# A second Strassen level inside two of the seven products of an MLP's first matrix product, for four pairs of output blocks

## The chip, the cores and the metric

The kernel runs on one core of one Trainium2 chip. The metric is the device time of one execution in microseconds (us). The engines are named as in the profile: PE (TensorE matmuls), PEld (its weight loads), DVE (VectorE), ACT (ScalarE), POOL (GpSimd) and SP (SyncE, which issues all DMAs here). DVE, ACT, POOL and SP each work through one list of instructions in the order of the program; an instruction waits until the semaphores it names have come, and what stands behind it on the same engine waits with it.

## The reference

One encoder layer on 1024 tokens of width 1024. Attention and a short convolution come first; the change lies in the last line.

```python
u = rms_norm(x, norm1_g); proj = u @ w_in          # q k v cb cc ch ga gb
...                                                # neighbourhood attention, gated conv, branches, gates
x = x + merged @ w_o                               # (1024, 1024)
h = rms_norm(x, norm2_g) @ w_mlp_in                # (1024, 4096)   "first MLP product"
x = x + jnp.square(jax.nn.relu(h)) @ w_mlp_out     # (1024, 1024)   "second MLP product"
```

Inputs and outputs are float32. A float32 operand is split into a high and a low float16 half, and a product is done in three passes (high·high, high·low, low·high; `PASSES`).

## The kernel before

**Strassen.** The first MLP product is computed as a 2x2 block product by a form of Strassen with seven products instead of eight. The tokens are cut into two halves of 512, the 1024 inner columns into two halves of 512, and the 4096 outputs into two halves of 2048. The seven forms of the activations (`fv`, `U2`, made once per 128 tokens by `sums`, `high`, `low` and DMA transposes) are shared by 16 blocks `q` of 128 + 128 output channels. For each block the weights (two raw tiles of 512 KB) become seven forms as well:

1. `rows_scaled`: ACT multiplies the raw rows by the norm's gain (8 instructions, in place); `squares`: two ACT squares with a row sum.
2. `sum_of`: DVE sums the two columns and casts the result into a column of `ones`; PE multiplies it by a matrix of ones (`all_sum`, line 227, a matmul with one column, to which the text refers as the *ones matmul*), and DVE makes a power-of-two scale of it (`pow2_half`).
3. `forms_sum`: POOL adds four weight forms (`tsum`); `forms_split` with `parts`: ACT writes the high halves (line 1238), DVE the low halves (line 1234) into `P1[q]`, one of three rotating buffers (`TAGS`).
4. `quad(q)`: seven groups of 4 x 3 matmuls of 128x512, each into one of the eight PSUM banks (`anybank` takes them in turn), 84 matmuls per block. DVE and ACT read the banks back into `AS[q]` (lines 1740 to 1761).
5. `h_done(q)`: ACT relu and square (2048 columns each), POOL four sums, and a store of 1.8 MB to the DRAM tensor `HS`.

Blocks 0 and 1 run in two halves of 256 tokens, since the last activation forms are still being made.

**What sets the order.** Python generators. `unit` emits a group of matmuls, then steps the foreground list `fg` (`step`) and the background list `bg` (`tick`) a few times; each `yield` gives the place to the next. So one fixed order per engine comes out of the interleaving. `gate(q)` holds back the writing of a weight buffer until the block that used it has been emitted, and `apart` keeps a ones matmul some matmuls behind its operand in the program. `X1` holds the residual, 128 x 8 x 1024 float32, and stays in place until the second MLP product adds to it.

Of the kernel before, what the change touches and what calls it, by code (L numbers as in the profile page):

```python
# [18 lines left out]
D = 1024  # L19
# [80 lines left out]
def encoder_block(ctx: ExitStack, tc: tile.TileContext, x, weights, cols, gqk, rel, masks, out):  # L100
# [282 lines left out]
    g1, g2, gm2 = at(consts, 0, 8), at(consts, 20, 8), keep()  # L383
    rows = {"A": lambda j: rowsA, "B": lambda j: rowsB, "O": lambda j: rowsM}
    chunks, offset = {}, 0
    for (kind, j), pieces in plan():
        ch = chunks[kind, j] = Chunk(kind, [(nk, sum(n for _, n in cs)) for _, _, nk, cs in pieces],
                                     {"A": "wa", "B": "wb"}.get(kind, "ws"), rows.get(kind, lambda j: g1)(j),
                                     j if kind == "V" else None, 9 if kind in "VQKCGS" else 0)
        ch.first = len(loads)  # L390
        for p, (k, w) in enumerate(ch.widths):
            ch.offs.append(offset)
            if kind != "X" and (kind, j) != ("1", 0) and (kind, j, p) != ("1", 1, 1):
                loads.append((ch, p))
            offset += 128 * k * w
# [1031 lines left out]

    pair_done, fv, ssq = [0], [], keep(10)

# [6 lines left out]
    def row_scale(col, n=1):  # L1436
        y = tmp(n)
        for _ in rstd(at(ssq, col, n), D, y, 9):
            pass
        return y  # L1440
# [5 lines left out]
    def begin(n):  # L1446
# [5 lines left out]
        for i in range(2):  # L1452
            normal(n + 4 * i, at(y, i))

    PART = ((0, 4), (4, 7))
# [62 lines left out]
    def prep1(q):  # L1518
# [7 lines left out]
        ready.add(q)  # L1526
        if 1 < q < 15:
            yield from sums1(q + 1)

    SQJ = U2[1][:, 0, :, :, 384:512].rearrange("p s k t -> p (s k) t").bitcast(BF16)  # L1530
# [20 lines left out]
    def forms_m():  # L1551
# [101 lines left out]
    def do(f, *a):  # L1653
        return lambda: f(*a)
# [12 lines left out]
    tail(3, 0, sq(6), do(low, 1, 0), lambda: y.append(row_scale(4, 2)), do(high, 1, 1),  # L1667
         lambda: (normal(2, at(y[0], 0)), normal(6, at(y[0], 1))), do(low, 1, 1))
# [3 lines left out]
    tail(7, 1, sq(3, 1), g1, lambda: normal(3, row3(3)), g1)  # L1672
    fv[1] = wsp.tile([128, 7, 2, 512], F16, name="v16", tag="ws")

    def last_pair():
# [51 lines left out]
    def quad(q, c0=0, c1=512):  # L1727
        need(q)
        if c0 == 0:
            while q - 2 in live:  # L1730
                step()
            live.add(q)
            AS[q] = w4p.tile([128, 7, 512], F32, name="as", tag="as")
        ps = {}
# [17 lines left out]
        def post3(ps):  # L1752
# [9 lines left out]
            7: post7, 3: post3}, 2 if c1 == 512 else 3, 5, (1, 2, 5, 4, 6, 7, 3) if c0 else (1, 6, 5, 4, 2, 7, 3))  # L1762

    def whole(q):
        quad(q)
        pe_done[0] = q + 1
# [9 lines left out]
    held[0] = 0  # L1776
    for q in range(2, 14):
        whole(q)


# [109 lines left out]
    bg.append(prep2(0))  # L1890
    whole(14)
    pace[0] = 1
    whole(15)
# [133 lines left out]
```

## Time and profile before

| | |
|---|---|
| median of 3 runs | 1201.6 us (1201.53 to 1202.12) |
| profiled execution, its own time | 1201.36 us |
| its span on the core | 1199.6 us, so 1.8 us lie around the span |
| granted TensorE clock | 1.00 |
| busy: PE, DVE, ACT, POOL | 1190.7, 937.1, 752.1, 450.5 us |
| instructions | 16983, of them 6272 matmuls |

The trace is of one execution. A busy PE is no proof of a PE at its peak, since matmuls overlap in the pipeline: the distance between the starts of two groups tells what a group costs. A row of the timeline gives start, length, engine, line, operation, output and inputs with their shapes, and behind it in brackets the time that the engine sat idle before it and who released it.

### The profile page before, as it was taken

To read this page: it belongs to the slowest core of one execution; us is meant where nothing else is said; L and a number is where in the kernel's file an instruction comes from. 1 tells how busy PE (TensorE), PEld (TensorE's weight loads), DVE (VectorE), ACT (ScalarE), POOL (GpSimd) and SP (SyncE) were. 2 spreads that over 40 slices of the span, in tenths; PEclk is the share of its full clock that TensorE was granted. 3 is DMA by queue.
4 is the path that set the end of the run, shared out by engine and by line. 5 is a ranking of instruction groups with operands and counts; after the bars stand their busy time and mean duration, and the time that the engine had idled before them with its cause. 6 is when DMAs were issued, how large, how long until landed. Compare 5 with 4: busy or idle time off the path is not lost.

```text
span 1199.6 us, 16983 instructions
## 1 busy us (share of the span) xinstructions
PE 1190.7 (99%) x6272; PEld 575.5 (48%) x6272; DVE 937.1 (78%) x1750; ACT 752.1 (63%) x1181; POOL 450.5 (38%) x296
## 2 busy tenths in 40 slices
PE   8999999999999999999999999999999999999998
PEld 7444444445444444444467444444444444444444
DVE  7987878899558786877888645645648999999998
ACT  7765668778654544336778778778575843746440
POOL 5610022322321213001014666565567561554562
PEclk9999999999999999999999999999999999999999
DMA  7745547687641121233396545535466925335302
GB/s 262 197 154 125 110 96 143 123 163 128 131 119 56 51 71 36 71 132 149 68 168 195 172 146 184 166 125 192 157 238 223 354 72 207 144 130 204 105 36 105
DMA packets 162707, 171.25 MB, mean 143 GB/s; under 512 B 123328, under 2 KB 123840, under 8 KB 158528
## 3 DMA queue, kind: packets, MB, share of 16 engines
q1 hardware_dynamic: 162624, 170.17, 48.7%
q8 instruction: 49, 0.80, 0.3%
q14 instruction: 34, 0.28, 0.1%
HBM read 102.51 MB, written 37.75 MB: 117 GB/s over the span
## 4 chain that ended last, share of the span: by engine, by line
PE 91%; DVE 6%; ACT 1%; issue 1%; DMA 1%; SPq 0%; DVEq 0%; ACTq 0%
PE ps_d L236 27%; PE ps_s L236 24%; PE ps_o L236 20%; PE ps_d L1067 11%; PE ps_d L669 2%; PE ps_d L718 2%; PE ps_s L718 2%; PE ps_s L669 2%; PE ps_o L1048 1%; PE ps_s L972 1%; DVE w_s L1234 1%; DVE sg L1357 1%; DMA xt<-in_x 1%; ACT w_s L1238 0%; DVE sc L362 0%
## 5 line engine op out<-in xcount | busy, mean ns | idle before, releaser
L236 PEld LDWEIGHTS <-ops 128*128 128x128 f16 x1356 | 132.4, 98 | 157.3
L236 PEld LDWEIGHTS <-w 128*128 128x128 f16 x1368 | 132.8, 98 | 139.5
L1067 PE MATMUL ps_d<-uT,w_ws 128*128 128x512 f16 x576 | 127.8, 379 | 0.0
L236 PE MATMUL ps_s<-ops 128*128 128x512 f16 (+1 forms) x516 | 115.7, 374 | 0.0
L236 PE MATMUL ps_d<-ops 128*128 128x512 f16 x492 | 112.9, 379 | 0.0
L236 PE MATMUL ps_d<-u2T,w 128*128 128x512 f16 (+1 forms) x504 | 110.1, 371 | 0.0
L1847 ACT ACTIVATE ops<-hf,sc 128x2048 f16<-128x2048 f32 x26 | 52.0, 1999 | 84.8 <-PE ps_d L236 47.1
L1221 POOL TENSOR_TENSOR tsum<-raw 128x512 f32<-128x512 f32 x28 | 48.2, 1737 | 139.4 <-DVE v L1475 73.9
L1425 POOL TENSOR_TENSOR as<-as 128x512 f32<-128x512 f32 x60 | 82.9, 1382 | 41.6 <-ACT as L1707 38.1
L236 PEld LDWEIGHTS <-w_s 128*128 128x128 f16 x588 | 56.8, 98 | 69.0 <-DVE w_s L1234 1.3
L1067 PEld LDWEIGHTS <-w_ws 128*128 128x128 f16 x576 | 54.6, 98 | 65.2 <-issue 1.0
L236 PE MATMUL ps_o<-ops 128*128 128x512 f16 x348 | 79.8, 379 | 0.0
L236 PE MATMUL ps_s<-u2x,w 128*128 128x512 f16 (+1 forms) x348 | 78.6, 375 | 0.0
L1849 DVE SCALAR_TENSOR_TENSOR ops<-hf,sc,ops 128x2048 f16<-128x2048 f32 x26 | 73.9, 2843 | 3.2 <-ACT ops L1847 2.2
L1099 ACT ACTIVATE raw<-raw,sc 128x256 f32<-128x256 f32 x164 | 67.5, 493 | 1.9 <-DMA raw<-in_weights 1.9
L1221 POOL TENSOR_TENSOR gsum<-raw 128x512 f32<-128x512 f32 x14 | 19.2, 1390 | 128.0 <-issue 53.6
L1238 ACT ACTIVATE w<-raw,sc 128x512 f16<-128x512 f32 (+1 forms) x28 | 24.6, 927 | 51.2 <-DVE sc L475 51.2
L1740 DVE TENSOR_TENSOR as<-ps_s,as 128x512 f32<-128x512 f32 x13 | 9.0, 692 | 57.9 <-ACT as L1759 57.9
L1321 ACT ACTIVATE sg<-sg,sc 128x2048 f32<-128x2048 f32 (+1 forms) x7 | 13.2, 1880 | 52.2 <-DVE sg L1319 52.2
L1863 POOL TENSOR_TENSOR raw<-raw 128x1024 f32<-128x1024 f32 x8 | 30.8, 3873 | 37.1 <-DVE ops L1857 37.1
L236 PE MATMUL ps_o<-u2T,w 128*128 128x512 f16 (+1 forms) x204 | 44.2, 366 | 0.0
L236 PEld LDWEIGHTS <-mH 128*128 128x128 f16 x304 | 29.6, 98 | 30.4
(393 smaller groups left out, 2663.0 us busy)
## 6 DMA issues: line engine op xcount, KB each, us to landing
raw<-in_weights SPq DMA_DIRECT2D x89, 512.0 KB, 5.2
hs<-as SPq DMA_DIRECT2D x16, 1792.0 KB, 8.7
hf<-hs SPq DMA_DIRECT2D x26, 1024.0 KB, 6.6
w2x<-in_weights SPq DMA_DIRECT2D x16, 512.0 KB, 7.5
raw<-in_weights SPq DMA_DIRECT2D x16, 384.0 KB, 3.5
xt<-in_x SPq DMA_DIRECT2D x8, 512.0 KB, 10.6
gs<-s SPq DMA_DIRECT2D x4, 1024.0 KB, 4.4
x<-in_x SPq DMA_DIRECT2D x8, 512.0 KB, 10.2
```

Of the source, the lines that this page charges most:

```text
L236: T.matmul(ps, l, r, start=a, stop=b)
L669: T.matmul(ps, UT[:, sa, k, b * 128:(b + 1) * 128], w, start=(kind, k) == ("hh", 0), stop=(kind, k) == ("hl", 7))
L718: T.matmul(vbank["q", b], UT[:, sa, k, b * 128:(b + 1) * 128], cQ.parts[:, sw, 512 * k:512 * k + 512], start=(k, n) == (0, 0), stop=(k, n) ...
L1067: T.matmul(ps, l, r, start=a, stop=b)
L1099: A.activation(v, v, AF.Copy, scale=sc[:, at(g, 4 * i + k)])
L1221: G.tensor_tensor(t[:, o], a, b, op=OP.add)
L1238: A.activation(o(0), w, AF.Copy, scale=sc[:, s])
L1321: A.activation(sg[:, :c], sg[:, :c], AF.Sigmoid, scale=sc[:, cS[n].inv])
L1425: sub.tensor_tensor(z[o], z[a], z[b], op=op)
L1847: A.activation(P[:, 1, 0], hf, AF.Copy, scale=sc[:, Rs])
L1849: V.scalar_tensor_tensor(P[:, 1, 1], hf, sc[:, Rs], P[:, 1, 0], op0=OP.mult, op1=OP.subtract)
L1863: G.tensor_tensor(w11[i2], w11[i2], w12[i2], op=OP.add)
```

## The change

Blocks 6 to 13 are taken in four pairs (6,7), (8,9), (10,11), (12,13). Of the seven products of the two blocks, those with the first activation form times the first weight form, and with the second times the second (`SEVEN` 1 and 2), are no longer computed for each block alone. Both blocks' product 1 together is a single matrix product with the channels of both blocks side by side, and it goes through a second level of seven products of half the inner length and 256 tokens (class `Level`, groups M1 to M7); the same with product 2. A `Level` has 7 x 2 x 3 = 42 matmuls of 128x256. The other five products of each block (`reg`) stay as they were, so a pair has 120 matmuls of 128x512 and 84 of 128x256, where two blocks had 168 of 128x512.

The second level needs activation sub-forms, and weight sub-forms for each pair. `subforms` runs once, in the foreground, after the last activation transposes: it stores `X1` to the new DRAM tensor `XS` (4 stores of 1 MB), scales four rows of `X1` in place, makes the sub-forms in the other half of `X1`, splits them and has SP transpose them into `SUB`, which lies in `X1` as well. `X1` is loaded back after block 14's product has been emitted. A third `AS` buffer (`AS3`) and a small weight piece also live in `X1`. `pairs_prep` replaces the preparation of blocks 6 to 13: rows and squares of both blocks, two scales and their ratios, the forms, and the sub-forms (eight POOL operations of 256 columns), in two steps, `pair_first` and `pair_second`. The odd pairs' raw weights have a buffer of their own, loaded by `pair_raws`.

```diff
+    APART = {("1", q) for q in (8, 9, 12, 13)}
...
-        if 1 < q < 15:
+        if 1 < q < 15 and q != Q0 - 1:
             yield from sums1(q + 1)
+    Q0, NPAIR = 6, 4
+    PAIR = {}
+    XS = dram.tile([128, 8, D], F32, name="xs")
+    XF = X1.rearrange("p b d -> p (b d)")
+    AS3 = XF[:, :3584].rearrange("p (f t) -> p f t", f=7)
+    SUB = XF[:, 4096:].bitcast(F16).rearrange("p (h s f k t) -> p h s f k t", h=2, s=4, f=2, k=2)
+    def subforms():
+        for b in range(0, 8, 2):
+            SP.dma_start(XS[:, b:b + 2], X1[:, b:b + 2])
+            yield from wait(4)
+        for b in range(4):
+            A.activation(X1[:, b], X1[:, b], AF.Copy, scale=sc[:, yrow[b]])
+            yield
+        S = [X1[:, 4 + 2 * b:6 + 2 * b].rearrange("p r (s f c) -> p (r s) f c", s=2, f=2) for b in range(2)]
+        V16 = [X1[:, b].bitcast(F16) for b in range(4)]
+        for b in range(2):
+            (a11, a12), (a21, a22) = ([X1[:, r].rearrange("p (f h c) -> p h f c", f=2, h=2)[:, h] for h in range(2)]
+                                      for r in (b, b + 2))
+            s1, s2, s3, s4 = (S[b][:, i] for i in range(4))
+            for o, x_, y_, op in ((s1, a21, a22, OP.add), (s2, s1, a11, OP.subtract), (s3, a11, a21, OP.subtract),
+                                  (s4, a12, s2, OP.subtract)):
+                V.tensor_tensor(o, x_, y_, op=op)
+                yield
+            s = X1[:, 4 + 2 * b:6 + 2 * b].rearrange("p r c -> p (r c)")
+            A.activation(V16[b], s, AF.Copy)
+            yield
+            V.tensor_tensor(V16[b + 2], s, V16[b], op=OP.subtract)
+            yield
+        for b in range(2):
+            for h in range(2):
+                SP.dma_start_transpose(SUB[:, h].rearrange("p s f k t -> p (s f k) t")[:, :, 128 * b:128 * b + 128],
+                                       V16[b + 2 * h])
+                yield from wait(3)
...
+    def pair_rows(p):
+        for q in (Q0 + 2 * p, Q0 + 2 * p + 1):
+            yield from rows_scaled(c1[q], g2)
+            PAIR["sm", q] = yield from squares(c1[q], t2.rearrange("p a c -> p (a c)").bitcast(BF16))
+    def pair_scales(p):
+        q = Q0 + 2 * p
+        am = [sum_of(PAIR.pop(("sm", q + j))) for j in range(2)]
+        yield
+        s = []
+        for j in range(2):
+            one, c1[q + j].inv = yield from scale_of(am[j], 9, 1)
+            s.append(one)
...
+    def pair_first(p):
...
+        for j, ch in enumerate((a, b)):
+            for _ in forms_sum(ch, PAIR["sums"][:, j], None):
+                pass
+            yield
...
+        for f in range(2):
...
+                G.tensor_tensor(o, u, v, op=op)
+            yield
+    def pair_second(p):
...
+        yield from gate(q + 1)
...
+        slots = [(P[:, 7], a.r[0][:, 1]), (R_[:, 0], a.r[0][:, 0]), (R_[:, 1], b.r[0][:, 1]), (R_[:, 7], a.r[1][:, 0])]
...
+        todo = [(2, 3, b.r[1][:, 1:2]), (3, 5, t[:, 0:2]), (5, 7, t[:, 2:4])]
+        yield from parts([((lambda i, w=w: w[:, i]), s) for w, s in slots], s2, lambda n: None)
+        yield from parts([((lambda i, j=j: half(E, j)[:, i]), b.r[j][:, 0, 256:]) for j in range(2)], s2,
+                         lambda n: None)
+        ready.add(q)
+        yield from parts([((lambda i, a=a, b=b: R_[:, a:b, i]), w) for a, b, w in todo], sb, lambda n: None)
+        ready.add(q + 1)
...
+    def pairs_prep():
+        yield from pair_rows(0)
+        yield from pair_scales(0)
+        pair_raws(1)
+        for p in range(NPAIR):
+            yield from pair_first(p)
+            if p + 1 < NPAIR:
+                yield from pair_rows(p + 1)
+            yield from pair_second(p)
+            if p + 1 < NPAIR:
+                yield from pair_scales(p + 1)
+        yield from sums1(14)
...
         bg.append(sums1(2))
-        bg.extend(prep1(q) for q in range(2, 16))
+        bg.extend(prep1(q) for q in range(2, Q0))
+        bg.append(pairs_prep())
+        bg.extend(prep1(q) for q in range(14, 16))
...
+        fg.append(subforms())
...
+    def pair(q):
+        need(q), need(q + 1)
...
+        class Level:
...
+            def post(self, z, base=None):
+                M, (zq_, zr_), t = self.M, z, self.t
+                def stt(o, i, c, y):
+                    V.scalar_tensor_tensor(o, i, c, y, op0=OP.mult, op1=OP.add)
+                A.activation(t[:, L], M[1], AF.Copy)
+                A.activation(t[:, H], M[1], AF.Copy, scale=rab)
+                stt(zr_[:, L], M[6], rb, t[:, H])
+                stt(zr_[:, H], M[7], rb, zr_[:, L])
+                V.tensor_tensor(zq_[:, L], M[2], t[:, L], op=OP.add)
+                A.activation(t[:, H], zr_[:, H], AF.Copy, scale=rba)
+                stt(zr_[:, L], M[5], rb, zr_[:, L])
+                stt(zr_[:, H], M[5], rb, zr_[:, H])
+                stt(zq_[:, H], M[4], ra, t[:, H])
+                stt(zr_[:, L], M[3], rb, zr_[:, L])
+                if base:
+                    for o, y in zip(z, base):
+                        G.tensor_tensor(o, o, y, op=OP.add)
+            def emit(self, then):
+                unit(self.mms((1, 6, 7, 2)), None, 2, 5)
+                unit(self.mms((5, 4, 3)), then, 2, 5)
...
+        one = Level(0, zr[1])
+        def end1():
+            one.post(z4)
+        one.emit(end1)
+        reg(q, 6, lambda: post6(q, zq))
+        reg(q, 5, lambda: post5(q, zq))
+        reg(q, 4)
+        reg(q, 7, lambda: post7(q, zq))
+        two = Level(1, zr[2])
+        two.emit(lambda: two.post(z0, z4))
+        def end2():
+            post3(q, zq)
+            fg.append(h_done(q, 0, 512, 2, 0))
+        reg(q, 3, end2)
+        pe_done[0] = q + 1
+        reg(r, 6, lambda: post6(r, zr))
+        reg(r, 5, lambda: post5(r, zr))
+        reg(r, 4)
+        reg(r, 7, lambda: post7(r, zr))
+        def end3():
+            post3(r, zr)
+            fg.append(h_done(r, 0, 512))
+        reg(r, 3, end3)
+        pe_done[0] = r + 1
...
-    for q in range(2, 14):
+    for q in range(2, Q0):
         whole(q)
+    for p in range(NPAIR):
+        pair(Q0 + 2 * p)
...
     whole(14)
+    SP.dma_start(X1[:, 4:8], XS[:, 4:8])
+    while 13 in live:
+        step()
+    SP.dma_start(X1[:, 0:4], XS[:, 0:4])
```

In `pair_first` the lines left out are the seven forms of `P1[q]`, as before. In `Level` they are the banks and the groups M1 to M7, each of two inner slices and three passes.

On DVE the order moves at two places of which the prediction speaks. The first is in the second halves of blocks 0 and 1, from the reading of the ones matmul's bank for block 2's scale (L230) on: before, the scale, the last bank of block 1's first half (`as_6167<-ps_d`), block 2's low halves and the next bank follow one another.

```order
L230 TENSOR_SCALAR sc_71<-ps_o_6255 128x1 [waits PE_49]
L469 TENSOR_SCALAR sc_71<-sc_71 128x1 [waits DVE_49]
L471 TENSOR_SCALAR sc_71<-sc_71 128x1 [waits DVE_49]
L473 TENSOR_SCALAR sc_71<-sc_71 128x1 [waits DVE_49]
L475 TENSOR_SCALAR sc_71<-sc_71 128x1 [waits DVE_49]
L476 TENSOR_SCALAR sc_71<-sc_71 128x1
L1753 TENSOR_TENSOR as_6167<-ps_d_6257,as_6167 128x256 [waits PE_49]
L1234 SCALAR_TENSOR_TENSOR w16_1_6293<-raw_5715,sc_71,w16_1_6293 128x512 [waits DMAHW0_49,Activation_49]
```

In the changed program the operations of `subforms` (L1557) stand among these rows and ahead of the first of them; DMAHW1 is the semaphore of the third store to `XS`.

```order
L1557 TENSOR_TENSOR x1_5394<-x1_5394 128x512 [waits DMAHW1_49,Activation_49]
L230 TENSOR_SCALAR sc_71<-ps_o_6262 128x1 [waits PE_49]
L1557 TENSOR_TENSOR x1_5394<-x1_5394 128x512 [waits DVE_49]
L470 TENSOR_SCALAR sc_71<-sc_71 128x1 [waits DVE_49]
L1557 TENSOR_TENSOR x1_5394<-x1_5394 128x512
L472 TENSOR_SCALAR sc_71<-sc_71 128x1 [waits DVE_49]
L474 TENSOR_SCALAR sc_71<-sc_71 128x1 [waits DVE_49]
L476 TENSOR_SCALAR sc_71<-sc_71 128x1 [waits DVE_49]
L477 TENSOR_SCALAR sc_71<-sc_71 128x1
L1904 TENSOR_TENSOR as_6169<-ps_d_6266,as_6169 128x256 [waits PE_49]
L1557 TENSOR_TENSOR x1_5394<-x1_5394 128x512
L1235 SCALAR_TENSOR_TENSOR w16_1_6306<-raw_5718,sc_71,w16_1_6306 128x512 [waits DMAHW0_49,Activation_49]
```

Some rows further on DVE, behind block 2's low halves, come the rest of `subforms` and then the banks of block 0's second half (`as_6027`).

```order
L1562 TENSOR_TENSOR x1_5394<-x1_5394 128x2048 [waits DMAHW0_49,DVE_49]
L1557 TENSOR_TENSOR x1_5394<-x1_5394 128x512 [waits DMAHW2_49]
L1912 TENSOR_TENSOR as_6027<-ps_o_6320,as_6027 128x256 [waits PE_49,Activation_49]
L1557 TENSOR_TENSOR x1_5394<-x1_5394 128x512 [waits DVE_49]
L1557 TENSOR_TENSOR x1_5394<-x1_5394 128x512
L1557 TENSOR_TENSOR x1_5394<-x1_5394 128x512 [waits DVE_49]
L1562 TENSOR_TENSOR x1_5394<-x1_5394 128x2048 [waits Activation_49]
```

So ten operations on `X1` now stand on DVE between the reading of banks, behind a wait for a store.

The second place is on DVE in block 5, at the cast (into `ones_72`) for the scale of the next weights. Before, it stands right behind the first bank operation of block 5 (L1740).

```order
L1753 TENSOR_TENSOR as_6844<-ps_o_6963,as_6844 128x512 [waits PE_49]
L1740 TENSOR_TENSOR as_6993<-ps_s_7010,as_6993 128x512 [waits DMAHW3_49,PE_49,Activation_49]
L1079 TENSOR_REDUCE sc_71<-sc_71 128x1
L1080 CAST ones_72<-sc_71 128x1 [waits DVE_49]
L1745 TENSOR_TENSOR as_6993<-ps_o_7026,as_6993 128x512 [waits PE_49]
```

In the changed program the casts for blocks 8 and 9 stand behind the low halves of `pair_second` of blocks 6 and 7 (L1235), and PE's ones matmul that reads the first of them stands ahead of block 5's last product.

```order
L1235 SCALAR_TENSOR_TENSOR w16_1_7098<-raw_6686,sc_71,w16_1_7098 128x512 [waits Activation_49]
L1235 SCALAR_TENSOR_TENSOR x1_5394<-raw_6688,sc_71,x1_5394 128x256 [waits Activation_49]
L1896 TENSOR_TENSOR as_7045<-ps_d_7102,as_7045 128x512 [waits DVE_49,PE_49]
L1235 SCALAR_TENSOR_TENSOR x1_5394<-raw_6830,sc_71,x1_5394 128x256 [waits DMAHW1_49,Activation_49]
L1235 SCALAR_TENSOR_TENSOR w16_1_7098<-raw_6830,sc_71,w16_1_7098 128x512 [waits Activation_49]
L1235 SCALAR_TENSOR_TENSOR w16_1_7098<-tsum_7003,sc_71,w16_1_7098 128x2x512 [waits Activation_49] x2
L1080 TENSOR_REDUCE sc_71<-sc_71 128x1
L1081 CAST ones_72<-sc_71 128x1 [waits DVE_49]
L1080 TENSOR_REDUCE sc_71<-sc_71 128x1
L1081 CAST ones_72<-sc_71 128x1 [waits DVE_49]
L1912 TENSOR_TENSOR as_7045<-ps_d_7148,as_7045 128x512 [waits PE_49]
```

The cast has moved from the start of the preparation of one block to the end of the preparation of a pair. On ACT, between the square of block 0's first half (L1707) and the copy of the first bank of its second half (L1759), the program had block 2's high halves alone:

```order
L1707 ACTIVATE as_6026,sc_71<-as_6026,sc_71 128x4x256 [waits Activation_49]
L1238 ACTIVATE w16_1_6293<-raw_5715,sc_71 128x512 [waits DVE_49]
L1238 ACTIVATE w16_1_6293<-raw_6023,sc_71 128x2x512
L1238 ACTIVATE w16_1_6293<-tsum_6124,sc_71 128x2x512 [waits Pool_49] x2
L1759 ACTIVATE as_6026<-ps_s_6279 128x256 [waits PE_49]
```

In the changed program four scalings of `X1` stand ahead of them (the waits are for the first two stores), and a copy of 2048 columns among them:


```order
L1852 ACTIVATE as_6027,sc_71<-as_6027,sc_71 128x4x256 [waits Activation_49]
L1547 ACTIVATE x1_5394<-x1_5394,sc_71 128x1024 [waits DMAHW7_49]
L1547 ACTIVATE x1_5394<-x1_5394,sc_71 128x1024
L1547 ACTIVATE x1_5394<-x1_5394,sc_71 128x1024 [waits DMAHW0_49]
L1547 ACTIVATE x1_5394<-x1_5394,sc_71 128x1024
L1239 ACTIVATE w16_1_6306<-raw_5718,sc_71 128x512 [waits DVE_49]
L1560 ACTIVATE x1_5394<-x1_5394 128x2048 [waits DVE_49,Activation_49]
L1239 ACTIVATE w16_1_6306<-raw_6024,sc_71 128x2x512
L1239 ACTIVATE w16_1_6306<-tsum_6125,sc_71 128x2x512 [waits Pool_49] x2
L1910 ACTIVATE as_6027<-ps_s_6291 128x256 [waits PE_49]
```

The bank that L1910 frees is the one into which PE writes the second product of block 1's second half.

More of the change, by code (lines that the diff above doesn't have):

```diff
@@ L1436, in row_scale @@
     def row_scale(col, n=1):
-        y = tmp(n)
+        y = keep(n)
         for _ in rstd(at(ssq, col, n), D, y, 9):
@@ new lines, in pair_raws @@
+    def pair_raws(p):
+        q = Q0 + 2 * p
+        if p % 2:
+            if "raw" not in PAIR:
+                PAIR["raw"] = wsp.tile([128, 4, 1024], F32, name="raw2", tag="ws")
+            for j in range(2):
+                c1[q + j].raw = [PAIR["raw"][:, 2 * j + i] for i in range(2)]
+                for i in range(2):
+                    load_into(c1[q + j].raw[i], c1[q + j], i)
+    def pair_rows(p):
+        for q in (Q0 + 2 * p, Q0 + 2 * p + 1):
+            yield from rows_scaled(c1[q], g2)
+            PAIR["sm", q] = yield from squares(c1[q], t2.rearrange("p a c -> p (a c)").bitcast(BF16))
@@ L1729, in quad @@
         if c0 == 0:
[L1730 to L1733, printed above, removed]
+            if q < 14:
+                while q - 2 in live:
+                    step()
+                live.add(q)
+                AS[q] = w4p.tile([128, 7, 512], F32, name="as", tag="as")
+            else:
+                while HELD[q] in live:
+                    step()
+                live.add(q)
+                AS[q] = w4p.tile([128, 7, 512], F32, name="as", tag="as")
         ps = {}
```

111 lines of the change are left out of this document (104 added, 7 removed).

## The prediction

> **What bounds the kernel now.** I read the page first (busy times, then the chain that ended last), then PE's timeline, and then, around the places where the order moves, the timelines of DVE, ACT, POOL and SP.
>
> ```profile
> PE 1190.7 (99%) x6272; PEld 575.5 (48%) x6272; DVE 937.1 (78%) x1750; ACT 752.1 (63%) x1181; POOL 450.5 (38%) x296
> PE 91%; DVE 6%; ACT 1%; issue 1%; DMA 1%; SPq 0%; DVEq 0%; ACTq 0%
> ```
>
> PE is the bound, and in the chain 91% of the span is its own. So the time changes by what the change takes from PE's stream, and by what it makes PE wait. PE's timeline gives the price of a group as the distance between two starts (columns: start, length).
>
> ```profile
> 640.73 1.47 PE L236 MATMUL ps_o<-u2x,w 128*128 128x256 f16 x12
> 642.04 1.47 PE L236 MATMUL ps_d<-u2T,w 128*128 128x256 f16 x12
> 643.35 1.47 PE L236 MATMUL ps_s<-u2T,raw 128*128 128x256 f16 x12
> ...
> 645.97 0.17 PE L227 MATMUL ps_d<-ones 128*128 128x1 bf16 x1
> ...
> 651.24 2.75 PE L236 MATMUL ps_d<-u2T,w 128*128 128x512 f16 x12
> 653.83 2.75 PE L236 MATMUL ps_s<-u2x,w 128*128 128x512 f16 x12
> ...
> 669.39 2.75 PE L236 MATMUL ps_d<-u2T,w 128*128 128x512 f16 x12
> ...
> 716.06 0.17 PE L227 MATMUL ps_s<-ones 128*128 128x1 bf16 x1
> ```
>
> Twelve matmuls of 256 columns take 1.31 us, twelve of 512 take 2.59 us; a block of seven groups takes 18.15 us (651.24 to 669.39). The two rows L227 are ones matmuls. Their operands come from DVE:
>
> ```profile
> 639.19 0.42 DVE L1761 TENSOR_TENSOR as<-ps_o,as 128x256 f32<-128x256 f32 x1
> 645.57 0.16 DVE L1080 CAST ones<-sc 128x1 bf16<-128x1 f32 x1
> 651.45 2.47 DVE L1234 SCALAR_TENSOR_TENSOR w<-tsum,sc,w 128x1024 f16<-128x1024 f32 x2
> 713.69 0.16 DVE L1080 CAST ones<-sc 128x1 bf16<-128x1 f32 x1
> ```
>
> Block 3's weights are complete at 653.9 and first used at 669.39: 15 us of cover. The ones matmuls have next to none: the cast ends at 645.73 and PE takes it at 645.97 (0.24 us), in the steady blocks 713.85 against 716.06 (2.2 us). PE runs its list in order, so a cast that comes later than that stops everything behind it. That is the narrow place.
>
> **What it takes away.** Two blocks are 14 groups of 2.59 = 36.26 us; a pair is 10 of 2.59 and 7 of 1.31 = 35.07 us. Four pairs save 4 x 1.19 = **4.8 us**. The 256-column price is from the same operands' rows, so I take it without a range.
>
> [...] The rows above say 109 and 216 ns, so I go by them.
>
> **The first stop: sub-forms in blocks 0 and 1.** Prices and positions before:
>
> ```profile
> 618.88 2.87 DVE L1425 TENSOR_TENSOR form<-form 128x512 f32<-128x512 f32 x4 [1.21 <-ACT form L1443]
> 607.03 2.29 DVE L1475 TENSOR_TENSOR v<-form,v 128x2048 f16<-128x2048 f32 x1
> 605.08 1.91 ACT L1470 ACTIVATE v<-form 128x2048 f16<-128x2048 f32 x1 [0.59 <-ACT u2x L1433]
> 633.80 1.76 ACT L1238 ACTIVATE w<-raw,sc 128x512 f16<-128x512 f32 x2 [2.63 <-DVE sc L475]
> 635.47 2.17 ACT L1238 ACTIVATE w<-tsum,sc 128x1024 f16<-128x1024 f32 x2
> 637.55 0.36 ACT L1759 ACTIVATE as<-ps_s 128x256 f32<-128x256 f32 x1
> 628.40 4.63 SPq L1476 DMA_TRANSPOSE u2x<-v  x1
> 633.13 4.14 SPq L259 DMA_DIRECT2D raw<-in_weights  x4
> 634.00:638.00 4.00, 4.00 (x39) 3.59 (x37) 3.31 (x5) 4.00 (x6) 0.00 (x0) 1.00 1.05 319
> ```
>
> SP is busy with transposes until 633; behind them come block 3's two raw loads and then the stores to XS. So ACT, free at 631.2 (633.80 less 2.63), sits at the first scaling of X1 until a store has landed, and DVE sits from about 633 at its first addition until the third has. Up to that store SP has sent 1 + 3 MB, 4.2 million bytes; at the 319 GB/s of the last row they take 13.1 us from 634: 647. [...]
>
> From 647 on, by the rows: three additions of 0.72 and the scale's small operations (0.9) to 650.1; block 1's last bank and a fourth addition to 651.2. ACT begins block 2's high halves at 650.1, takes the 2048-column copy from 651.2 to 653.1, ends the high halves (1.05 + 2.17) at 656.4 and frees the bank with L1759's copy at 656.7; PE wanted that bank at 643.35. It cannot go on far: DVE ends the low halves at 657.9 and does 2.29 + 0.72, the bank (0.42), three additions, then waits for ACT's second copy (1.9): 665.4; 2.3 for the second subtraction, four sums and six bank operations of 0.42 (4.0) and the cast: 672.0. The ones matmul of 645.97 runs at 672.1: **26 us**. Bounds: were the stores free, DVE's ten new operations alone are 8 x 0.72 + 2 x 2.29 = 10.3 us ahead of a cast with 0.24 us to spare: 10. With each store 4.4 us by itself (the row of `gs`, below) the third lands at 651: 30.
>
> ```profile
> gs<-s SPq DMA_DIRECT2D x4, 1024.0 KB, 4.4
> ```
>
> Block 2's and 3's weights are late by less than PE is, so nothing more is added there. The four transposes into SUB and the late loads for block 4 lie under these 26 us and the two blocks after.
>
> **The second stop: entry into the pairs.** A block on ACT and POOL now:
>
> ```profile
> 684.86 3.29 ACT L1099 ACTIVATE raw<-raw,sc 128x256 f32<-128x256 f32 x8
> 688.05 1.04 ACT L1108 ACTIVATE tsum<-raw 128x1024 f32<-128x1024 f32 x1
> 690.29 1.91 ACT L1705 ACTIVATE as<-as 128x2048 f32<-128x2048 f32 x1
> 692.23 2.00 ACT L1707 ACTIVATE as<-as,sc 128x2048 f32<-128x2048 f32 x1
> 694.24 0.57 ACT L1759 ACTIVATE as<-ps_d 128x512 f32<-128x512 f32 x1
> ...
> 704.72 3.33 POOL L1221 TENSOR_TENSOR tsum<-raw 128x512 f32<-128x512 f32 x2 [4.99 <-ACT raw L1099]
> 708.60 2.62 POOL L1221 TENSOR_TENSOR tsum<-tsum,raw 128x512 f32<-128x512 f32 x2 [0.56 <-ACT tsum L1108]
> 712.47 5.30 POOL L1425 TENSOR_TENSOR as<-as 128x512 f32<-128x512 f32 x4 [1.24 <-ACT as L1707]
> ```
>
> Rows and squares of a block are 3.2 + 2.5 = 5.8 us of ACT (684.86 to 690.29, less what lies between), relu and square 4.1, high halves 3.9. The ones matmul for blocks 8 and 9 stands before the last group of block 5, and its cast behind the whole of `pair_second` of blocks 6 and 7. From the end of block 5's high halves (684.86) to there PE needs 2.6 + 18.15 + 15.5 = 36.3 us. ACT has ahead of it: rows and squares of four blocks 23.2, relu and square of two 8.2, copies 1.1, block 6's high halves 3.9, the second set (four of 512, two of 256, one of 512, two of 1024) 6.5: 42.9, and DVE's last low half and cast 1.6. So 8 us are missing if ACT never waits. It waits: 1.8 for the scales, 3.6 for POOL, which does four sums (5.3) and four forms (5.95) ahead of ACT's halves of the forms, and 4.2 for block 4's last bank, which DVE reads behind those low halves: **18 us**. Ends 8 and 22 (another set of POOL forms, 4, in the way).
>
> **The third: each pair with another behind it.** The same cast must come before the pair's last group. PE from one such ones matmul to the next: 35.1 us. ACT: relu and square of two blocks 8.2, six copies of 256 columns 2.2, high halves 3.9 + 6.5, rows and squares of two blocks 11.6: 32.4, beginning 4.9 after the ones matmul (the last group, its bank); with DVE's tail 38.9, so 3.8 missing. ACT's halves of the forms again stand behind POOL's sums (5.3) and forms (5.95), by 7 us: **11 us**, ends 4 and 14, for two pairs (the one before the last has no rows to do, and is 11.6 us lighter). POOL itself has 10.6 + 11.9 + 8 short and 2 long additions, about 31 of 35 us. Nothing else holds PE: the sub-form slots are read after the same cast; X1 comes back 36 us ahead of the second product.
>
> **Sum.** -4.8 + 26 + 18 + 22 = +61.2 on the profiled execution's 1201.36 (0.2 under the median 1201.6): **1262.6**.
>
> **Rivals.**
> - *The cover holds (faster).* If ACT, DVE and POOL do their new work in the gaps and no cast is late, 1201.4 - 4.8 = 1196.6. For it: 15 us of cover for weights, ACT idle 37%. Against: the casts' 0.24 and 2.2 us; it decides at whether a cast ends before PE reaches its ones matmul. 0.09.
> - *Only the first stop counts.* If POOL and ACT keep pace in the pairs: 1201.4 - 4.8 + 26 = 1222.6. 0.14.
> - *The stores cost little, the pairs stop.* DVE's own work alone: 1201.4 - 4.8 + 10 + 40 = 1246.6. 0.12.
> - *Short matmuls that don't hide their loads.* A load of 98 ns laid bare on each of 336 would add 33 us and, alone, give 1229.6. [...] 0.02.
>
> My forecast has 0.61; 0.02 is left for neither way. That the change doesn't do what it says is closed: the order has the 84 short matmuls per pair.
>
> **Numbers.** All cases but the first are slower. The low end is -4.8 + 10 + 8 + 8 = +21 (1222.6), with the second rival's spread 1218; the high end -4.8 + 30 + 22 + 28 = +75, 1277. About 0.2% (2.4 us) is what a measurement of this kernel tells from no change: faster 0.09, same 0.02, slower 0.89.
>
> **What would show it.** Right: PE idle from about 641, released by DVE and ACT, in sum 20 to 30 us before block 2; DMA as the releaser of ACT's first L1547 and DVE's first L1557; then PE waiting for DVE's cast (L1081) at block 5's last group, 13 us or more, and at the last group of blocks 7 and 9. Pairs at 46 us, the last two at 35. Wrong: ACT's L1547 starting before 640, a cast ahead of PE in blocks 5, 7 and 9, or groups of 256 columns off 1.31 us.

## The result, and the profile after

The changed kernel takes 1295.65 us (median of 5 runs, 1295.18 to 1297.79) against 1201.6 us, a ratio of 1.0785 (95% interval 1.0772 to 1.0797). The prediction had the sign and its three places, but the time lies above its range (1218 to 1277). The profiled execution took 1297.79 us, with a span of 1296.0 us, 96.4 more than before.

The page: busy times, the granted clock in 40 slices, and the chain that ended last.

```profile
PE 1205.5 (93%) x6416; PEld 594.8 (46%) x6416; DVE 1010.9 (78%) x1860; ACT 774.7 (60%) x1223; POOL 494.8 (38%) x336
PEclk9999999999999999999969979789899999999999
PE 59%; DVE 17%; ACT 9%; issue 6%; POOL 5%; DMA 3%; SPq 0%; DVEq 0%; POOLq 0%; ACTq 0%
```

PE has fewer columns to compute and is yet busy for 14.8 us more. The second row tells why: its clock, 1.00 over the span before, falls to 0.6 to 0.8 in five slices. The longest of PE's waits (releaser; us in total, times, longest):

```profile
PE ps_o L227 <- DVE sc L1080: 30.4, 2, 17.3
PE ps_d L227 <- DVE ones L1081: 13.4, 2, 11.7
PE ps_d L227 <- DVE sc L1080: 12.7, 1, 12.7
PE ps_o L236 <- DVE sc L230: 7.7, 1, 7.7
PE ps_d L236 <- DVE as L1983: 5.7, 1, 5.7
PE ps_d L236 <- DVE ops L2123: 4.0, 1, 4.0
```

The casts (L1080, L1081) hold most of it, as forecast; before, all of PE's waits together were under 5 us. PE's timeline at the stops and at the starts of blocks and pairs (block 2 at 683.21, pair 0 at 777.08, the next pairs at 827.82, 878.74 and 914.35, block 14 at 958.86, the second product at 995.14):

```profile
649.31 2.72 PE L236 MATMUL ps_o<-u2x,w 128*128 128x256 f16 x12 [7.71 <-DVE sc L230]
675.12 0.19 PE L227 MATMUL ps_d<-ones 128*128 128x1 bf16 x1 [11.69 <-DVE ones L1081]
675.17 2.72 PE L236 MATMUL ps_s<-u2T,t 128*128 128x256 f16 x12
683.21 2.75 PE L236 MATMUL ps_d<-u2T,w 128*128 128x512 f16 x12
...
772.54 0.16 PE L227 MATMUL ps_o<-ones 128*128 128x1 bf16 x1 [17.26 <-DVE sc L1080]
772.57 4.68 PE L236 MATMUL ps_d<-u2x,w 128*128 128x512 f16 x12
777.08 0.82 PE L236 MATMUL ps_s<-u2T,w 128*128 128x256 f16 x6
...
822.83 0.16 PE L227 MATMUL ps_d<-ones 128*128 128x1 bf16 x1 [12.68 <-DVE sc L1080]
827.82 0.82 PE L236 MATMUL ps_d<-u2T,w 128*128 128x256 f16 x6
873.64 0.16 PE L227 MATMUL ps_o<-ones 128*128 128x1 bf16 x1 [13.11 <-DVE sc L1080]
878.74 0.90 PE L236 MATMUL ps_s<-u2T,w 128*128 128x256 f16 x6
...
924.82 5.28 PE L236 MATMUL ps_d<-u2x,w 128*128 128x512 f16 x12 [5.72 <-DVE as L1983]
```

Behind these stops the first groups take up to twice their time: the twelve long matmuls at 772.57 need 4.51 us instead of 2.59, the twelve short ones at 675.17 need 2.51 instead of 1.31. The windows show the granted clock there (columns: window, length, busy times of PE, PEld, DVE, ACT, POOL, clock, DMA share, GB/s):

```profile
675.17:677.70 2.53, 2.53 (x14) 1.78 (x15) 1.47 (x9) 2.50 (x5) 0.00 (x0) 0.50 1.15 207
772.57:777.08 4.51, 4.51 (x13) 1.62 (x13) 3.38 (x11) 0.00 (x0) 0.00 (x0) 0.56 0.45 177
777.08:778.40 1.32, 1.32 (x14) 1.18 (x13) 0.69 (x1) 0.39 (x1) 0.00 (x0) 1.00 0.00 0
```

The bill, from the distances between those starts, less what the same work takes without a stop (before: 36.74 for blocks 0 and 1, 18.15 per block, 35.07 for a pair: 10 groups of 2.59 and 14 half groups of 0.655). "Idle" is the sum of the waits in brackets (first stop 7.71 + 3.27 + 1.79 + 11.69, entry 1.72 + 17.26, pair 0 0.24 + 12.68, pair 1 13.11, pairs 2 and 3 0.27 + 5.72 + 0.75, second product 0.86 + 4.03), "slow clock" is what is left of the loss.

| place | forecast | idle | slow clock | loss |
|---|---|---|---|---|
| blocks 0 and 1 (first stop) | 26 | 24.5 | 6.8 | 31.3 |
| blocks 4 and 5 (entry) | 18 | 19.0 | 2.3 | 21.3 |
| pairs 0 and 1 | 22 | 26.0 | 5.5 | 31.5 |
| pairs 2 and 3 | 0 | 6.7 | 3.2 | 10.0 |
| short matmuls | -4.8 | | | -5.0 |
| second MLP product and end | 0 | 4.9 | 1.7 | 6.6 |
| start of the first product | 0 | | | 0.7 |
| sum | 61.2 | | | 96.4 |

Not all of the column "slow clock" is the clock's doing. Of the 17.8 us in the first product, the groups behind the last stop of each place took 12.3 us longer than at full clock (2.8, 1.9, 4.9 and 2.7). Another 3.3 us are such groups inside the first stop; they delayed nothing, since PE stood waiting afterwards for a cast, and DVE waited for ACT and DMA alone on its way there (648.50 to 674.91). The last 2.2 us are the overlap of neighbouring groups (0.16 us), which each stop undoes.

What held DVE and ACT at the first stop, as forecast the stores (ACT, then DVE):

```profile
643.52 2.19 ACT L1547 ACTIVATE x<-x,sc 128x1024 f32<-128x1024 f32 x2 [11.14 <-DMA xs<-x]
648.50 0.69 DVE L1557 TENSOR_TENSOR x<-x 128x512 f32<-128x512 f32 x1 [14.84 <-DMA xs<-x]
661.48 0.42 DVE L1912 TENSOR_TENSOR as<-ps_o,as 128x256 f32<-128x256 f32 x1
661.81 4.77 DVE L1557 TENSOR_TENSOR x<-x 128x512 f32<-128x512 f32 x3
674.91 0.16 DVE L1081 CAST ones<-sc 128x1 bf16<-128x1 f32 x1
```

And the chain that makes pair 0 long: POOL's sums for HS, then its weight sums, ACT waiting for these, at the end DVE's low halves and the cast.

```profile
782.12 5.31 POOL L1426 TENSOR_TENSOR as<-as 128x512 f32<-128x512 f32 x4 [22.65 <-ACT as L1852]
787.40 2.48 POOL L1222 TENSOR_TENSOR tsum<-raw 128x512 f32<-128x512 f32 x2
789.91 1.15 ACT L1239 ACTIVATE w<-tsum,sc 128x1024 f16<-128x1024 f32 x1 [3.94 <-POOL tsum L1222]
793.80 1.15 ACT L1239 ACTIVATE w<-tsum,sc 128x1024 f16<-128x1024 f32 x1 [2.74 <-POOL tsum L1222]
805.59 0.18 ACT L1109 ACTIVATION_READ_ACCUMULATOR t<-raw 128x1 f32 x1
818.64 3.88 DVE L1235 SCALAR_TENSOR_TENSOR w<-tsum,sc,w 128x1024 f16<-128x1024 f32 x2
822.62 0.16 DVE L1081 CAST ones<-sc 128x1 bf16<-128x1 f32 x1
```

The squares that the cast sums up are ready at 805.8; the cast comes at 822.6.

### The profile page after: what moved, and what is told of

Its sections match the earlier page's. It is cut to its first block, busy times and chain, and to the rows that moved or that the text cites. A ratio compares the mean times of both kernels' runs of the same rounds, so it can differ in the third digit from the quotient of the medians.

```text
span 1296.0 us, 17489 instructions
## 1 busy us (share of the span) xinstructions
PE 1205.5 (93%) x6416; PEld 594.8 (46%) x6416; DVE 1010.9 (78%) x1860; ACT 774.7 (60%) x1223; POOL 494.8 (38%) x336
## 4 chain that ended last, share of the span: by engine, by line
PE 59%; DVE 17%; ACT 9%; issue 6%; POOL 5%; DMA 3%; SPq 0%; DVEq 0%; POOLq 0%; ACTq 0%
PE ps_d L236 17%; PE ps_s L236 16%; PE ps_o L236 13%; PE ps_d L1068 5%; POOL tsum L1222 2%; DVE w L1235 2%; ACT raw L1100 2%; PE ps_d L670 2%; PE ps_d L719 2%; PE ps_s L719 2%; DVE P L95 1%; PE ps_s L670 1%; POOL as L1426 1%; DVE w_s L1235 1%; ACT w L1239 1%
## 5 line engine op out<-in xcount | busy, mean ns | idle before, releaser
L236 PEld LDWEIGHTS <-w 128*128 128x128 f16 x1464 | 145.6, 100 | 189.6 <-issue 74.5
L1426 POOL TENSOR_TENSOR as<-as 128x512 f32<-128x512 f32 x48 | 69.8, 1454 | 78.8 <-ACT as L1852 76.0
L1068 PEld LDWEIGHTS <-w_ws 128*128 128x128 f16 x576 | 54.6, 98 | 65.7 <-issue 1.5
L236 PE MATMUL ps_d<-u2T,w 128*128 128x512 f16 (+1 forms) x336 | 69.4, 356 | 0.0
L1235 DVE SCALAR_TENSOR_TENSOR w<-raw,sc,w 128x512 f16<-128x512 f32 (+1 forms) x40 | 47.7, 1216 | 21.2 <-ACT w L1239 21.2
L236 PE MATMUL ps_s<-u2x,w 128*128 128x512 f16 (+1 forms) x264 | 61.7, 385 | 0.0
L1850 ACT ACTIVATE as<-as 128x2048 f32<-128x2048 f32 (+1 forms) x14 | 25.0, 1782 | 42.5 <-DVE as L1904 27.2
L236 PE MATMUL ps_s<-u2T,w 128*128 128x512 f16 (+1 forms) x258 | 48.0, 333 | 0.0
L1235 DVE SCALAR_TENSOR_TENSOR w<-tsum,sc,w 128x1024 f16<-128x1024 f32 x28 | 46.5, 1692 | 0.4
L236 PE MATMUL ps_o<-u2x,w 128*128 128x512 f16 (+1 forms) x168 | 37.2, 374 | 8.2 <-DVE sc L230 7.7
```

The costliest lines, as they stand in the source:

```text
L236: T.matmul(ps, l, r, start=a, stop=b)
L1068: T.matmul(ps, l, r, start=a, stop=b)
L1235: V.scalar_tensor_tensor(o(1), w, sc[:, s], o(0), op0=OP.mult, op1=OP.subtract)
L1426: sub.tensor_tensor(z[o], z[a], z[b], op=op)
L1850: A.activation(v[:, 0:4], v[:, 0:4], AF.Relu)
```

## The experiments

Each kernel but one was timed in three rounds beside the kernel before. The lengths of the stages in their traces, worked out as above from the starts of PE's groups. They are from one execution each, and that of the changed kernel took 2.1 us more than its median; differences of that size between rows say little:

| kernel | median, us | ratio, 95% interval | blocks 0, 1 | 2 to 5 | pair 0 | pair 1 | pair 2 | pair 3 |
|---|---|---|---|---|---|---|---|---|
| before | 1201.6 | | 36.7 | 72.6 | 36.3 | 36.3 | 36.3 | 36.3 |
| changed | 1295.65 | 1.0785 (1.0772 to 1.0797) | 68.0 | 93.9 | 50.7 | 50.9 | 35.6 | 44.5 |
| sub-forms, no pairs | 1233.72 | 1.0263 (1.0248 to 1.0278) | 68.0 | 72.6 | 36.3 | 36.3 | 36.3 | 36.3 |
| the same without stores | 1219.25 | 1.0140 (1.0123 to 1.0157) | 54.8 | 72.6 | 36.3 | 36.3 | 36.3 | 36.3 |
| sub-forms late | 1283.33 | 1.0680 (1.0662 to 1.0698) | 36.7 | 111.8 | 50.5 | 50.8 | 35.6 | 44.5 |
| casts behind the squares | 1289.82 | 1.0731 (1.0715 to 1.0747) | 67.5 | 82.6 | 54.6 | 45.4 | 42.5 | 42.3 |
| casts in the middle | 1286.70 | 1.0706 (1.0688 to 1.0724) | 67.3 | 93.3 | 44.6 | 47.0 | 35.5 | 45.0 |
| POOL sums first | 1280.82 | 1.0655 (1.0639 to 1.0671) | 66.2 | 94.9 | 44.7 | 44.7 | 35.8 | 39.0 |
| both of these | 1272.05 | 1.0584 (1.0568 to 1.0600) | 67.1 | 91.9 | 40.4 | 41.9 | 35.1 | 42.1 |
| all three moves | 1258.18 | 1.0467 (1.0451 to 1.0482) | 36.7 | 108.6 | 38.7 | 43.8 | 35.1 | 40.1 |
| and a later second pair | 1264.71 | 1.0520 (1.0504 to 1.0536) | 36.7 | 91.7 | 61.6 | 43.6 | 35.1 | 40.4 |

### The first stop alone

```diff
-        bg.extend(prep1(q) for q in range(2, Q0))
-        bg.append(pairs_prep())
-        bg.extend(prep1(q) for q in range(14, 16))
+        bg.extend(prep1(q) for q in range(2, 16))
...
-    for q in range(2, Q0):
-        whole(q)
-    for p in range(NPAIR):
-        pair(Q0 + 2 * p)
+    for q in range(2, 14):
+        whole(q)
```

> The activation sub-forms are made where the change makes them, but blocks 6 to 13 are computed block by block as before, so the sub-forms are read by nobody. Theory (late casts and late bank reads at separate places, each of which adds its stop): only the first stop is left, 651.24 to 683.21 in the trace of the changed kernel, so 1201.6 + 32 = 1233.6 us, and blocks 2 to 15 take 18.15 us each. Rival (the sub-forms leave ACT and DVE behind, and that backlog feeds the later stops): blocks 2 to 5 or later ones show waits as well, and the time is above 1240.

1233.72 us. Blocks 0 and 1 take 68.0 us, and every later block 18.15: the first stop is worth 31 to 32 us and leaves nothing behind it in the first product, so the rival (a backlog that feeds the later stops) falls.

### What a stop costs beside its length

```diff
+        for _ in range(STOPS.get(t_of.get(id(ch)), 0)):
+            V.tensor_reduce(sc[:, tmp(1)], ch.raw[1], axis=AX, op=OP.add)
         ch.sum = sum_of(sm)
...
+    STOPS = {4: 3, 6: 5, 8: 7, 10: 10, 12: 14, 14: 18}
```

> The kernel before, with 3, 5, 7, 10, 14 and 18 row sums of 1024 columns on DVE put ahead of the cast in blocks 3, 5, 7, 9, 11 and 13, which makes PE stop there for growing times (about 1.1 us each less the 2.2 us of slack). It measures what a stop costs beside its own length. Theory: after a stop of several us PE runs at a granted clock of 0.50 for some us, whatever the length of the stop, so each longer stop costs 2 to 3 us more than itself and a short one nothing. Rival: the price grows with the length of the stop. The time is 1201.6 plus the stops (about 51 us) plus 8 to 15 us by the theory.

One run, 1261.32 us. PE's timeline at five of the stops, and the windows behind the first two of these:

```profile
702.62 0.16 PE L227 MATMUL ps_s<-ones 128*128 128x1 bf16 x1 [3.19 <-DVE ones L1080]
744.52 0.16 PE L227 MATMUL ps_s<-ones 128*128 128x1 bf16 x1 [5.43 <-DVE ones L1080]
792.01 0.16 PE L227 MATMUL ps_s<-ones 128*128 128x1 bf16 x1 [8.82 <-DVE ones L1080]
844.15 0.16 PE L227 MATMUL ps_s<-ones 128*128 128x1 bf16 x1 [13.33 <-DVE ones L1080]
900.34 0.16 PE L227 MATMUL ps_s<-ones 128*128 128x1 bf16 x1 [17.84 <-DVE ones L1080]
```

```profile
702.62:707.00 4.38, 4.38 (x22) 2.02 (x22) 3.40 (x15) 2.37 (x3) 0.00 (x0) 1.00 0.99 371
744.52:749.50 4.98, 4.98 (x14) 1.85 (x14) 1.28 (x7) 3.59 (x4) 0.00 (x0) 0.55 0.41 153
```

The five blocks last 21.51, 25.95, 29.48, 33.53 and 38.94 us. Less 18.15 and the stop, 0.17, 2.37, 2.51, 2.05 and 2.95 us remain, 0.16 of each being the overlap that a stop undoes. The stop of 3.2 us here cost only itself and left the clock at 1.00; from 5.4 us on each cost 2 to 3 us more, hardly growing with its length, and left the clock at 0.50 to 0.60 over the next 5 us. The three sums in block 3 delayed PE by 0.3 us. In total 10.8 us stand beside the stops, within the 8 to 15 of the theory. This is a term that the prediction lacked.

The traces of the other kernels show the same for long stops, but not a sharp threshold. Behind every stop of 3.6 us or more PE lost 1.3 to 2.9 us, without a trend up to 17.9 us. Stops that stand alone and last up to 2.3 us cost nothing. Between 2.5 and 3.6 us it goes either way. From the run with all three moves (below), two stops and the windows behind them:

```profile
678.00 4.20 PE L236 MATMUL ps_o<-u2T,w 128*128 128x512 f16 x12 [2.52 <-DVE as L1917]
793.67 0.18 PE L227 MATMUL ps_o<-ones 128*128 128x1 bf16 x1 [3.44 <-DVE sc L1080]
678.00:682.00 4.00, 4.00 (x13) 1.46 (x13) 4.00 (x2) 0.00 (x0) 3.69 (x2) 0.64 0.99 293
793.69:798.90 5.21, 5.21 (x26) 2.38 (x27) 5.19 (x5) 1.07 (x2) 5.21 (x4) 1.00 0.76 240
```

The stop of 2.52 us was followed by a slow clock (0.64; 1.7 us lost), the one of 3.44 us was not (1.00). Shortly behind a longer stop a shorter one counted once and once not: in the changed kernel the 3.27 us at 657.45 were followed by a clock of 0.50, and the group behind the 1.79 us at 661.96 took its usual 1.47 us. What decides in this range no run here shows.

How long the clock stays low can be estimated from the losses: at 0.50, the clock from 675.17 to 677.70 in the changed kernel, the 1.3 to 2.9 us lost are 2.6 to 5.8 us of running at it.

### The stores in the first stop

```diff
-        for b in range(0, 8, 2):
-            SP.dma_start(XS[:, b:b + 2], X1[:, b:b + 2])
-            yield from wait(4)
+        yield from wait(16)
```

> As the run that makes the sub-forms and computes all blocks one by one (1233.7 us), but the four stores of X1 and its loading back are left out, so that the residual that enters the last sum is destroyed. ACT's scaling and DVE's additions then wait for no store. Theory (the stores set the first stop down to DVE's own work): the stop falls from 31.3 us to the lower bound of the prediction, 10 us, and 2 to 3 for the lower clock behind it: 1201.6 + 13 = 1215. Rival (the extra work on ACT and DVE alone is enough to hold PE): 1225 or more.

1219.25 us, nearer to the theory's 1215 than to the rival's 1225. The stop is 54.84 - 36.74 = 18.1 us, 14.7 of it idle:

```profile
648.54 1.47 PE L236 MATMUL ps_o<-u2T,mH 128*128 128x256 f16 x12 [3.04 <-DVE as L1907]
661.71 0.18 PE L227 MATMUL ps_d<-ones 128*128 128x1 bf16 x1 [11.69 <-DVE ones L1081]
```

So the stores are worth 13 us of the 31, and DVE's new operations with the waits among them 14.7, not the 10 that I had as the lower bound. The last wait, 11.69 us, is as long as with the stores (675.12 above), so it is the work of DVE and ACT and not theirs. The bound of 10 left out three additions that take 4.77 us instead of 2.16 (as at 661.81 in the changed kernel) and DVE's waits for ACT, which is busy with its two copies (2.41 and 1.98 us).

### The sub-forms from block 2 on

```diff
-        fg.append(subforms())
+        fg.append(stores())
...
+    fg.append(subforms())
     for q in range(2, Q0):
```

> The four stores stay where they are, but the scaling and the sub-forms start with block 2, so that ACT and DVE do not wait for the stores. Theory: the first stop is gone and nothing takes its place, 1295.7 - 32 = 1263.7 us, block 2 starting at about 651. Rival (the work itself is too much, 8.2 us of ACT and 10.3 us of DVE must go somewhere): the stop moves into blocks 3 to 6, 1275 to 1290.

1283.33 us, the rival. Blocks 0 and 1 are back at 36.7 us, but blocks 2 to 5 have grown by 17.9. In block 3 DVE holds a bank behind the additions and low halves, and in block 4 a cast is late, since ACT waited 4.66 us for raw weights that SP issued behind the four transposes:

```profile
682.10 5.22 PE L236 MATMUL ps_o<-u2T,w 128*128 128x512 f16 x12 [6.31 <-DVE as L1904]
710.92 1.70 ACT L1100 ACTIVATE raw<-raw,sc 128x256 f32<-128x256 f32 x4 [4.66 <-DMA raw<-in_weights]
717.26 0.16 PE L227 MATMUL ps_d<-ones 128*128 128x1 bf16 x1 [6.71 <-DVE ones L1081]
```

### The casts right behind the squares

```diff
+    def pair_casts(p):
+        q = Q0 + 2 * p
+        PAIR["am", p] = [sum_of(PAIR.pop(("sm", q + j))) for j in range(2)]
...
                 yield from pair_rows(p + 1)
+                pair_casts(p + 1)
```

> The two casts for the next pair stand on DVE right behind that pair's squares, ahead of the low halves of the second step, instead of behind them; nothing else moves. Theory (the place of the cast is what stops PE): in the changed kernel the squares end 8.7 us (763.6 to 772.3) and 17 us (805.6 to 822.6) ahead of the casts, so the entry loses 8 us of its stop and a pair's stop falls from 15.8 to a few us, where the slots' weights come last: 1295.7 - 8 - 2 x 10 = 1268. Rival (the chain through ACT and POOL sets the pair's length and the cast only shows it): PE waits at the next pair's first weights instead, and the time is above 1288.

1289.82 us: my theory falls as stated, and the rival has the time but not the place, since PE did not wait at the next pair's first weights. Blocks 2 to 5 became 11 us shorter and pair 1 5.5, but pairs 0 and 2 became longer by 3.9 and 6.9. In pair 0 DVE reaches the second cast before ACT has done the square, and the reading of the banks stands behind it in the same queue; PE then stops for a bank (L1989) instead of a cast:

```profile
802.45 0.16 DVE L1080 TENSOR_REDUCE sc<-sc 128x1 f32<-128x2 f32 x1 [5.06 <-ACT t L1109]
804.76 5.28 PE L236 MATMUL ps_o<-u2x,w 128*128 128x512 f16 x12 [7.42 <-DVE as L1989]
```

The run doesn't tell whether ACT's and DVE's amount of work bounds a pair, or this one wait. The next runs ask that.

### The chain in a pair

Casts in the middle: `pair_casts` stands in `pair_second` ahead of the low halves of the second block.

```diff
         ready.add(q)
+        if p + 1 < NPAIR:
+            pair_casts(p + 1)
         yield from parts([((lambda i, a=a, b=b: R_[:, a:b, i]), w) for a, b, w in todo], sb, lambda n: None)
```

> As the changed kernel, but the two casts for the next pair stand ahead of the last three low halves of the second step (the forms of the pair's second block), not behind them; ACT's squares are long done there, so that DVE cannot be held up by the cast, as it was by 5.1 us in the run with the casts right behind the squares. Theory (a pair is one chain ACT, POOL, ACT, DVE that the cast closes; what is taken out of the chain comes off the pair): the casts come 6 us earlier in pairs 0 and 1 and 3 us at the entry: 1295.7 - 15 = 1281. Rival (DVE's own queue of bank reads and low halves is the limit, the cast only shows it): the stop moves to a bank, and the time stays above 1290.

1286.70 us, between the two. Pair 0 lost 6.1 us as forecast, pair 1 3.9, the entry 0.6 instead of 3. PE still waits for the cast there (7.75 and 8.27 us), not for a bank as the rival had it.

POOL sums first: the sums of a pair's first block are made ahead of its scales.

```diff
             yield from pair_second(p)
             if p + 1 < NPAIR:
+                first_sums(p + 1)
                 yield from pair_scales(p + 1)
```

> As the changed kernel, but POOL makes the four weight sums of a pair's first block right before the casts, ahead of its sums for HS in the next pair, so that ACT does not wait for them (3.9 and 2.7 us in pair 0). Theory (chain): pairs 0 and 1 lose 6.7 us each, the entry 3.3: 1295.7 - 17 = 1279. Rival (the sums only move and something else on POOL comes late by as much): above 1290.

1280.82 us, the theory: pairs 0 and 1 lost 6.1 and 6.2 us; the entry gained nothing, and pair 3 lost 5.5 that were not forecast, so that the whole time agrees partly by luck.

> Both of these together. Theory (chain): the two add up, 1295.7 - 32 = 1264, pairs 0 and 1 near 38 us. Rival (amount of work: ACT 30.7 and DVE 37 us busy in a pair's 50.7 leave no room below 45): 1275 or more.

1272.05 us. In pairs 0 and 1 the two moves nearly add up, to 40.4 and 41.9 us instead of 38; what is left of pair 0's stop:

```profile
807.67 0.18 PE L227 MATMUL ps_o<-ones 128*128 128x1 bf16 x1 [3.43 <-DVE sc L1080]
```

That ACT's and DVE's work leaves no room below 45 us is refuted; a pair was long because its work stood in one chain. The time is 8 us above the theory's: the pairs are 6 us longer than it had them, and the entry gained 2 us instead of 6.

> Both, and the sub-forms from block 2 on, with four steps instead of one between ACT's copy and DVE's subtraction of the sub-forms, so that DVE does not wait for ACT there (3.2 us in the run with late sub-forms). Theory: 12 us less than the run with both, as the late sub-forms gave alone, and a few more for the spreading: 1264 - 16 = 1248. Rival (backlog in blocks 2 to 5 adds to the entry): 1260 or more. Faster than the kernel before (1201.6) by neither.

1258.18 us, nearer to the rival (1260): the late sub-forms gave 14 us net (12 alone), and blocks 2 to 5 stay at 108.6, 36 us too long.

### The entry

```diff
             yield from pair_first(p)
-            if p + 1 < NPAIR:
+            if 0 < p < NPAIR - 1:
                 yield from pair_rows(p + 1)
             yield from pair_second(p)
+            if p == 0:
+                yield from gate(Q0 + 2)
+                yield from pair_rows(1)
+                pair_casts(1)
```

> As the run with all three moves (1258.2 us), but the rows, squares and casts of the second pair come behind the second step of the first pair, when block 5 has been emitted, instead of ahead of it; the ones matmul of the second pair then stands in the first pair, not ahead of block 5's last product. Theory (backlog on ACT: the work of four blocks' rows must be done before the second pair, wherever it is put): block 5's 16 us of stop become stops in pairs 0 and 1, the time moves by less than 6 us. Rival (only the place of the cast): the 16 us go, 1242.

1264.71 us, 6.5 us longer, just over the theory's 6. Block 5 runs without a stop, and pair 0 takes 61.6 us instead of 38.7, with two stops:

```profile
759.92 0.16 PE L227 MATMUL ps_d<-ones 128*128 128x1 bf16 x1 [8.83 <-DVE ones L1081]
800.30 0.16 PE L227 MATMUL ps_d<-ones 128*128 128x1 bf16 x1 [13.00 <-DVE sc L1080]
```

A later place for rows and casts does not win the 16 us, so the rival falls. The backlog on ACT is not shown either: ahead of the rows that were held back ACT sat idle for 9.93 and 8.66 us, waiting for DVE to read a bank (until 731.20 and 750.18), and the rows began at 752.00. The stops in pair 0 can as well come from this late start. In the run with all three moves ACT also waits 6.70 us for raw weights there (727.89). What makes the entry long is thus left open. None of the versions beats the kernel before: all that the short matmuls save is 5 us, and the smallest sum of stops reached is 61 (1258.2 - 1201.8 + 5).

## Why the prediction was wrong, by its own steps

- **The gain.** Right: 35.06 us for a pair without a stop in the run with both moves, 4 x 1.24 = 5.0 saved against 4.8. The price of 109 ns for 256 columns held (0.655 us for six), and with it the rival of the bare loads falls: weight loads took 98 ns each before too (`LDWEIGHTS` on PEld), and beside them the short matmuls started every 109 ns, not every 207.
- **The first stop.** The place and the releasers were right. The third store landed at 648.5, where DVE starts, against 647, and the cast ended at 675.07 against 672.0. The 26 us were the delay of the ones matmul; it was 28.4 (675.12 less 645.97 and the later start, 0.7), and 2.8 more were lost behind it at the slow clock: 31.3. The lower bound of 10 for DVE's work was too low (14.7 of idle time without the stores).
- **The entry.** Idle 19.0 against 18, partly by luck. ACT waited 1.6 us for the scales and 3.3 for POOL, as reckoned (1.8 and 3.6), but 7.9 instead of 4.2 for block 4's last bank. If the waits simply add up, about 6 of the 8 us that the step counted as missing work remain.
- **Pairs 0 and 1.** Idle 26.0 against 22, inside the ends of 4 to 14 each. POOL's sums held ACT for 6.7 us (reckoned 7), and the chain was the cause, as the two moves show.
- **The steps that failed** are two terms that the sum put at nothing.
  - *The clock.* The sum took the time that PE stands still as the whole price of a stop. The slow clock behind the stops added 12.3 us in the first product and 1.6 in the second. The granted clock of 1.00 in the kernel before was that of a PE that never waited over 1.4 us. So the trace before could not show the price; the run with the stops does (2.05 to 2.95 us from a stop of 5.4 us on).
  - *"The last two at 35" and "Nothing else holds PE".* Pair 2 is right (35.6), but pair 3 took 44.5: I had looked for late casts only, and DVE was late with a bank there (L1983, 5.72 us) and with block 14's cast (0.75). At the second product 6.6 us were lost, where ACT waited 7.4 us for a part of `HS` (`ops<-hs`) loaded behind the second half of `X1`. The run with sub-forms and no pairs, which loads `X1` back too, waits 1.7 us there, the one without stores and loading back not at all; more than that was not tried, so this cause is argued from the trace.

The 35.2 us between 61.2 and 96.4 are: pairs 2 and 3 and the second product 16.6; the slow clock behind the stops of the other three places 9.6; these stops themselves, longer than reckoned, 8.5 (2.5, 1.3 and 4.7); the later start 0.7; the gain -0.2. By these numbers neither failed term alone explains the miss: without the slow clock the time would be about 1282 us, without the stops in pairs 2 and 3 and the second product about 1279, both above the range; without both about 1269 (estimates from the bill).

## What to carry over

Price a stop of the matmul engine at its length plus what the clock takes behind it: here 1.3 to 2.9 us for every stop of 3.6 us or more, nothing for one that stands alone and lasts up to 2.3 us, and either between. In an in-order queue, look for every operation that PE waits for, bank reads as well as scales: a cast that is moved ahead can hold the banks behind it (7.42 us at L1989, in the run with the casts behind the squares). A saving of 5 us cannot carry a one-time preparation that must fit between engines which have 0.24 us (at the cast of 645.57) to 2.2 us (in the steady blocks) to spare.

## What was not expected of the hardware

Beside the clock: where POOL was at work some of DVE's operations took longer, others not. In the changed kernel one addition of two SBUF operands takes 0.69 us at 648.50 with POOL idle, and three of them 4.77 at 661.81, while POOL adds up weights (659.07 to 667.7); in the same stretch the addition at 660.88 takes 0.69, and L1912 at 661.48, with an operand in PSUM, its usual 0.42. Over all blocks the low halves have become slower by 29% (the groups of before and after; mean ns last before the idle time):

```profile
L1234 DVE SCALAR_TENSOR_TENSOR w<-tsum,sc,w 128x1024 f16<-128x1024 f32 x28 | 35.7, 1315 | 0.0
```

```profile
L1235 DVE SCALAR_TENSOR_TENSOR w<-tsum,sc,w 128x1024 f16<-128x1024 f32 x28 | 46.5, 1692 | 0.4
659.07 5.30 POOL L1222 TENSOR_TENSOR tsum<-raw 128x512 f32<-128x512 f32 x2 [26.14 <-ACT raw L1100]
```

Taken by place, two of these operations together last 2.5 us where POOL is busy for less than half of that time (13 of 14 places before, 7 of 14 after), and 3.5 to 4.5 us where it is busy for more than 70% of it (the one other place before, seven after; 818.64 above, 3.88 us, is one).

In these places DVE is slower where both work; no run took POOL away to test it, so that POOL is the cause is not shown. The prediction took DVE's prices from rows without this.
